# Sums over w_o rows for two tokens: accumulated in PSUM, half of them moved behind a second fetch of the weights

## The chip, the cores and the metric

One core of a Trainium2 chip runs the whole program. The metric is device microseconds of one execution, given as the median of several runs. Beside it stands one execution taken with the hardware profiler; all rows come from that one. Its engines are named PE (TensorE matmuls), PEld (TensorE weight loads), DVE (VectorE), ACT (ScalarE), POOL (GpSimd) and SP (the queue that starts most loads).

## The reference

A block of a streaming encoder works on 16 learned meta tokens followed by 512 tokens of x, with 1024 channels in float32. Two branches (stick-breaking attention and gated linear attention) are projected, gated, added and projected again:

```
mix = (gate_sb * (sb @ w_sb_out) + gate_gla * (o @ w_gla_out)) @ w_o
h = h + rmsnorm(mix)
```

A gated MLP follows, with a causal convolution over three tokens between `hn @ w_ffn_up` and the gelu. The meta tokens are dropped at the end. The convolution looks back two tokens, so of the 16 meta tokens the last two are needed after `mix`: 514 tokens in all.

## The kernel before

**Numbers in parts.** Every matmul operand is split into a high part and a low part (`split`, line 136, and `load_w`, line 80): ACT rounds the operand to the high part, and DVE or POOL subtracts it from the operand for the low part. Three matmuls (high-high, high-low, low-high) stand for one. `load_w` starts the transfer on SP into one of three "raw" buffers, casts on ACT (line 89) and subtracts on POOL (line 90). A raw buffer comes free when its last reader is done.

**Order of the work.** A planner orders the instructions of each engine from a model of their times, with the order of the program text as priority; on the chip each engine then keeps that order, and waits where an operand or buffer is late. An `issue_after` in the text pins an instruction behind another.

**The stretch around the change.** It starts after the attention stages.

1. Lines 783 to 794, for each of 8 slices j of 128 channels: the attention branch is projected (`proj`, 24 matmuls into one of two PSUM buffers of the tag "mm"), the result is multiplied by its gate (line 786), the other branch `tg` is added (line 787), and the mix is split into `mh[j]` and `ml[j]` (line 137 on ACT, 138 on DVE). Its first two columns, the two last meta tokens, are copied to `m2` (line 791). At odd j the rows of w_o for two slices, columns 512 to 1023, are loaded (`raw_o`) and split into `woh` and `wol`, which stay in SBUF.
2. Lines 884 to 892, the first half of the output projection: for the 512 tokens in four blocks and columns 0 to 511 of w_o, loaded two slices at a time (`raw_oa`), 96 matmuls into the same two "mm" buffers.
3. `second` (line 896): the upper half of the columns, 24 matmuls per token block into the tag "z". `gained` squares a result on ACT (line 821) and multiplies it by the norm's gain on DVE (line 822). `normed` (line 831) makes the two norms of a token block and transposes it by 16 matmuls (line 845) into PSUM tiles of the tag "s", of which there are two.
4. The two meta tokens do not go through these matmuls. `accumulate` (line 774) forms their products on DVE: for each of the 8 slices and each token a row of w_o, 128 x 512, is multiplied by the token's column of `m2` and added to `acc` in SBUF (line 779; the first one is line 781). That is 16 operations for columns 512 to 1023, in the loop of item 1, and 16 for columns 0 to 511, in the loop of item 2. `mini` (line 849) adds `acc` over the partitions by 32 matmuls (line 855) and makes the norms of these two tokens; it is pinned behind the matmuls of `second(3)`.
5. The loads of `w_ffn_up` and `w_ffn_gate` (`raw_up`, `raw_ga`) come next in the same three raw buffers; their first matmuls need the normed tokens.

Of the kernel before, what the change touches and what calls it, by code (L numbers as in the profile page):

```python
# [9 lines left out]
F32 = mybir.dt.float32  # L10
# [3 lines left out]
ALU = mybir.AluOpType  # L14
PSUM = bass.MemoryType.PSUM

P = 128
D = 1024
KT = D // P
NM = 16  # L20
# [3 lines left out]
T0 = 14  # L24
# [26 lines left out]
def block_kernel(ctx: ExitStack, tc: tile.TileContext, x, meta_tokens, norm_mix_pre, w_in, w_gk_up, b_gk,  # L51
# [3 lines left out]
    pe, act, dve, pool, sp = nc.tensor, nc.scalar, nc.vector, nc.gpsimd, nc.sync  # L55

    x = x[0]
    out = out[0]
    w_in, w_gk_up, w_sb_out, w_gla_out, w_o = w_in[0], w_gk_up[0], w_sb_out[0], w_gla_out[0], w_o[0]
# [6 lines left out]
    wp = ctx.enter_context(tc.tile_pool(name="wp", bufs=3))  # L66

    def mmt(name):
        return psm.tile([P, 1024], F32, tag="mm", name=name)

    def pst(name, tag="s"):
        return pss.tile([P, 512], F32, tag=tag, name=name)
# [5 lines left out]
    last_raw = [None]  # L78

    def load_w(src, nk, name, hi_out=None, lo_out=None, lo_eng=pool, into=None):  # L80

        ncol = src.shape[-1]
        raw = wp.tile([P, nk, ncol], F32, tag="raw", name=f"raw_{name}")
        sp.dma_start(raw, src)
        last_raw[0] = raw
        if hi_out is None:
            hi_out = (into or wp).tile([P, nk, ncol], F32R, tag="wh", name=f"wh_{name}", bufs=2)
            lo_out = (into or wp).tile([P, nk, ncol], F32R, tag="wl", name=f"wl_{name}", bufs=2)
        act.copy(hi_out, raw)  # L89
        lo_eng.tensor_tensor(out=lo_out, in0=raw, in1=f32(hi_out), op=ALU.subtract)  # L90
        return hi_out, lo_out

    def cols(w, c0, n=P):
        return w[:, c0 : c0 + n].rearrange("(k p) m -> p k m", p=P)

    def wrows(w, k0, nk, c0, c1):
        return w[k0 * P : (k0 + nk) * P, c0:c1].rearrange("(k p) m -> p k m", p=P)

    def proj(w, xh, xl, segs, name, apart=False):

        wh, wl = w
        nk, m = wh.shape[1], wh.shape[2]
        (l0, l1), (_, l2) = segs
        pt = mmt(f"pt_{name}")
        segs = [(pt[:m, 512 - l1 + l0 : 512], l0, l1), (pt[:m, 512 : 512 + l2 - l1], l1, l2)]
        steps = [(k, a, b) for k in range(nk) for a, b in ((wh, xh), (wh, xl), (wl, xh))]
        for grp in ([[s] for s in segs] if apart else [segs]):
            for n, (k, a, b) in enumerate(steps):
                for dst, lo, hi in grp:
                    pe.matmul(dst, a[:, k, :], b[:, k, lo:hi], start=n == 0, stop=n == len(steps) - 1)  # L110
        return pt[:m, 512 - l1 + l0 : 512 + l2 - l1]
# [24 lines left out]
    def split(hi, lo, src):  # L136
        act.copy(hi, src)  # L137
        last_low[0] = dve.tensor_tensor(out=lo, in0=src, in1=f32(hi), op=ALU.subtract)  # L138
# [194 lines left out]
    with ExitStack() as pgs:  # L333
# [4 lines left out]
        for h in LEVELS:  # L338
            with tc.issue_after(low4.ins) if h < EASY else ExitStack():
                m = pgc.tile([P, 264], F32, name=f"mk{h}")  # L340
# [24 lines left out]
        with tc.tile_pool(name="plr", bufs=2) as plr:  # L365
# [30 lines left out]
            for c, (t, n) in enumerate(CHUNKS):  # L396
# [4 lines left out]
                e = plr.tile([P, 512], F32, tag="e", name=f"e{c}", bufs=5)  # L401
# [181 lines left out]
    tg = pm.tile([P, 8, TQ], F32, name="tg")  # L583
    with tc.tile_pool(name="pa", bufs=1) as pa:
# [169 lines left out]
        gates, mh, ml = {}, {}, {}  # L754
# [16 lines left out]
    m2 = pr.tile([P, 8, NM - T0], F32, name="m2")  # L771
    acc = pr.tile([P, NM - T0, D], F32, name="acc")

    def accumulate(k0, c):
        for kk in range(2):
            for t in range(NM - T0):
                w, m = last_raw[0][:, kk, :], m2[:, k0 + kk, t : t + 1]
                if k0 + kk:
                    dve.scalar_tensor_tensor(out=acc[:, t, c], in0=w, scalar=m, in1=acc[:, t, c], op0=ALU.mult, op1=ALU.add)
                else:  # L780
                    dve.tensor_scalar(out=acc[:, t, c], in0=w, scalar1=m, scalar2=None, op0=ALU.mult)

    for j in range(8):
        e = pr.tile([P, TQ], F32, tag="e", name=f"mix{j}", bufs=2)
        pt = proj(load_w(cols(w_sb_out, j * P), 4, f"so{j}"), sbh, sbl, LATE, f"so{j}")
        dve.tensor_tensor(out=e, in0=pt, in1=gates[j], op=ALU.mult)
        dve.tensor_tensor(out=e, in0=e, in1=tg[:, j, :], op=ALU.add)
        mh[j] = pe_.tile([P, TQ], F32R, tag=f"mh{j}", name=f"mh{j}")
        ml[j] = pe_.tile([P, TQ], F32R, tag=f"ml{j}", name=f"ml{j}")
        split(mh[j], ml[j], e)  # L790
        dve.tensor_copy(m2[:, j, :], e[:, : NM - T0])
        if j % 2:
            load_w(wrows(w_o, j - 1, 2, 512, D), 2, f"o{j}", hi_out=woh[:, j - 1 : j + 1, :], lo_out=wol[:, j - 1 : j + 1, :])
            accumulate(j - 1, slice(512, D))
    p1.close()


# [11 lines left out]
    with tc.tile_pool(name="pw", bufs=1) as pw:  # L809
# [39 lines left out]
        def mini():  # L849

            nt = NM - T0
            tp = pst("mini")
            for k in range(KT):
                for t in range(nt):
                    pe.matmul(tp[:, nt * k + t : nt * k + t + 1], acc[:, t, k * P : (k + 1) * P], ones[:, 0:1], start=True, stop=True)
            z = tp[:, : nt * KT].rearrange("p (k t) -> p k t", t=nt)

            def rstd(src, nm):
                s = pw.tile([P, KT, nt], F32, tag="msq", name=f"msq{nm}")
                act.activation(s, src, AF.Square)  # L860
                tp = pst(f"ms{nm}")
                yield
                pe.matmul(tp[:, : nt * KT], ones, s.rearrange("p k t -> p (k t)"), start=True, stop=True)
                ss = pw.tile([P, nt], F32, tag="mss", name=f"mss{nm}")
                dve.tensor_reduce(out=ss, in_=tp[:, : nt * KT].rearrange("p (k t) -> p t k", t=nt), op=ALU.add, axis=mybir.AxisListType.X)
                return rstd_of(pw, ss, D, nm).unsqueeze(1).broadcast_to([P, KT, nt])

            h = pw.tile([P, KT, nt], F32, name="hm")
            dve.tensor_tensor(out=h, in0=z, in1=g1T.unsqueeze(2).broadcast_to([P, KT, nt]), op=ALU.mult)
            dve.tensor_tensor(out=h, in0=h, in1=(yield from rstd(z, "mix0")), op=ALU.mult)  # L870
            dve.tensor_tensor(out=h, in0=h, in1=mT.rearrange("p t k -> p k t"), op=ALU.add)
            g = pw.tile([P, KT, nt], F32, name="hmg")
            dve.tensor_tensor(out=g, in0=h, in1=g2T.unsqueeze(2).broadcast_to([P, KT, nt]), op=ALU.mult)
            dve.tensor_tensor(out=g, in0=g, in1=(yield from rstd(h, "ffn0")), op=ALU.mult)
            split(h2h[:, :, SEQ:], h2l[:, :, SEQ:], g)
            yield
# [4 lines left out]

        pos = [mmt("wo01"), mmt("wo23")]
        d0 = [pos[i // 2][:, (i % 2) * 512 : (i % 2) * 512 + 512] for i in range(4)]
        for k in range(8):
            if k % 2 == 0:
                wh, wl = load_w(wrows(w_o, k, 2, 0, 512), 2, f"oa{k}")
                accumulate(k, slice(0, 512))
            a, b = wh[:, k % 2, :], wl[:, k % 2, :]
            for i in range(4):
                t = slice(i * P + NM - T0, i * P + P + NM - T0)  # L890
                for q, (m, w) in enumerate(((mh, a), (mh, b), (ml, a))):
                    pe.matmul(d0[i], m[k][:, t], w, start=k == 0 and q == 0, stop=k == 7 and q == 2)  # L892

        last_mm = [None]

        def second(i):
            t = (i - 1) * P + NM - T0
            ops = [(m[k][:, t : t + P], w[:, k, :]) for k in range(8) for m, w in ((mh, woh), (mh, wol), (ml, woh))]
            pt = pst(f"wob{i}", "z")
            for q, (a, b) in enumerate(ops):  # L900
                after = sum(q >= c for c in CUT) if i == 4 else 0
                with tc.issue_after(last_ht[after].ins) if after else ExitStack():
                    last_mm[0] = pe.matmul(pt, a, b, start=q == 0, stop=q == len(ops) - 1)
            return pt
# [4 lines left out]
        m = mini()  # L909
        for i in (2, 3, 4):  # L910
            pt = second(i)
# [24 lines left out]
    with tc.tile_pool(name="pu", bufs=2) as pu:  # L936
        for m in range(FT):
            pt = proj(load_w(cols(w_up, m * P), KT, f"up{m}", into=wx if m % 2 else None), h2h, h2l, FFNS, f"up{m}", apart=m < 2)
# [8 lines left out]
            for r, d in ((1, 1), (0, 2)):  # L947
                c = cw[:, r, m : m + 1]
# [223 lines left out]
```

## Time and profile before

| what | us |
|---|---|
| median of 3 runs (968.11 to 970.13) | 969.35 |
| the profiled execution | 969.08 |
| its span, first to last instruction | 967.3 |

| engine | busy us | share of the span |
|---|---|---|
| PE | 938.5 | 97% |
| PEld | 866.3 | 90% |
| DVE | 661.5 | 68% |
| ACT | 488.9 | 51% |
| POOL | 357.6 | 37% |

The mean granted clock of TensorE over the span was 0.992 of full speed. The stretch of items 1 and 2 lies between 508 and 574 us of the span; mini's matmuls start at 586.74 and the first matmul of the MLP at 596.00. A busy share is a mean over all stages, so a stretch is read by its own rows: who is busy there, and what ended the others' idle time.

### The profile page before, as it was taken

What the parts mean: (1) busy time and instruction counts of PE and PEld (TensorE: products, weight loads), DVE (VectorE), ACT (ScalarE), POOL (GpSimd) and SP (SyncE); (2) the same over time, 40 slices, a digit from 0 to 9 for tenths busy, and PEclk for the clock granted to TensorE, in tenths of its full rate; (3) what the DMA queues carried; (4) which work ended last, traced back from release to release, by engine and by line L of the source; (5) the groups of instructions that cost most, each with busy time, mean ns of one, the idle gap of its engine ahead of it and who ended that gap; (6) DMA issues with size and microseconds to landing.
All of it is one profiled execution on the core that took longest, in us unless ns stands there. A gap on an engine that the chain in (4) does not pass through costs nothing.

```text
span 967.3 us, 16621 instructions
## 1 busy us (share of the span) xinstructions
PE 938.5 (97%) x6588; PEld 866.3 (90%) x6588; DVE 661.5 (68%) x1110; ACT 488.9 (51%) x913; POOL 357.6 (37%) x268
## 2 busy tenths in 40 slices
PE   7999999999999998999999899999999999999996
PEld 7999999999999998999998678998999999988775
DVE  6675867767557877777858967554545554478897
ACT  5664554546377565665754235433333333355654
POOL 6523232222244554444545452444444444200200
PEclk9999999999999999999999999999999999999999
DMA  7122212221222321232213364233333233364923
GB/s 216 45 66 66 66 45 66 66 66 44 67 66 67 86 68 45 65 88 58 75 55 90 117 207 140 61 112 93 89 92 104 87 88 94 103 237 167 254 86 127
DMA packets 129727, 92.79 MB, mean 96 GB/s; under 512 B 4064, under 2 KB 114914, under 8 KB 129650
## 3 DMA queue, kind: packets, MB, share of 16 engines
q1 hardware_dynamic: 126178, 82.55, 28.8%
q0 software_dynamic: 1504, 2.88, 1.8%
q10 hardware_dynamic: 1968, 6.29, 1.8%
q8 instruction: 52, 0.85, 0.4%
q14 instruction: 25, 0.20, 0.1%
HBM read 87.52 MB, written 4.19 MB: 95 GB/s over the span
## 4 chain that ended last, share of the span: by engine, by line
PE 83%; DVE 10%; issue 2%; ACT 2%; POOL 2%; DMA 1%; DVEq 0%; ACTq 0%; POOLq 0%
PE pt_up L110 13%; PE ga L958 13%; PE pt_gr L110 5%; PE pt_gv L110 5%; PE pt_go L110 4%; PE pt_mg L110 4%; PE dA L1020 3%; PE pt_ms L110 3%; PE dD L1020 3%; PE pt_gk L110 2%; PE dB L1020 2%; PE wo L892 2%; PE pt_gq L110 2%; PE pt_sv L110 2%; PE pt_sk L110 2%
## 5 line engine op out<-in xcount | busy, mean ns | idle before, releaser
L90 POOL TENSOR_TENSOR wl_up<-raw_up,wh_up 128x1024 fp32r<-128x1024 f32 x22 | 53.0, 2409 | 68.3 <-ACT wh_up L89 68.3
L90 POOL TENSOR_TENSOR wl_ga<-raw_ga,wh_ga 128x1024 fp32r<-128x1024 f32 x22 | 55.2, 2509 | 56.6 <-ACT wh_ga L89 56.6
L110 PE MATMUL pt_up<-h2l,wh_up 128*128 128x256 f32 (+1 forms) x352 | 73.6, 283 | 0.3 <-DVE h2l L207 0.2
L110 PE MATMUL pt_up<-h2h,wh_up 128*128 128x256 f32 (+1 forms) x352 | 73.6, 283 | 0.2
L110 PE MATMUL pt_up<-h2h,wl_up 128*128 128x256 f32 (+1 forms) x352 | 73.3, 282 | 0.0
L958 PE MATMUL ga<-h2h,wl_ga 128*128 128x512 f32 (+1 forms) x192 | 72.2, 376 | 0.0
L958 PE MATMUL ga<-h2l,wh_ga 128*128 128x512 f32 (+1 forms) x192 | 72.2, 376 | 0.0
L958 PE MATMUL ga<-h2h,wh_ga 128*128 128x512 f32 (+1 forms) x192 | 72.0, 375 | 0.0
L89 ACT CAST wh_up<-raw_up 128x1024 fp32r<-128x1024 f32 x22 | 23.0, 1049 | 85.8 <-PE pt_up L110 76.2
L110 PEld LDWEIGHTS pt_up<-h2h,wh_up 128*128 128x128 f32 x352 | 56.9, 189 | 2.2 <-ACT h2h L206 0.5
L110 PEld LDWEIGHTS pt_up<-h2l,wh_up 128*128 128x128 f32 x352 | 55.5, 189 | 0.7 <-DVE h2l L207 0.7
L110 PEld LDWEIGHTS pt_up<-h2h,wl_up 128*128 128x128 f32 x352 | 55.3, 189 | 0.0
L958 PEld LDWEIGHTS ga<-h2h,wl_ga 128*128 128x128 f32 x192 | 36.2, 189 | 7.0
L949 DVE SCALAR_TENSOR_TENSOR cy<-pt_up,cw,cy 128x511 f32<-128x511 f32 (+1 forms) x22 | 16.4, 745 | 37.7 <-ACT cy L946 37.7
L958 PEld LDWEIGHTS ga<-h2l,wh_ga 128*128 128x128 f32 x192 | 36.2, 188 | 6.2
L958 PEld LDWEIGHTS ga<-h2h,wh_ga 128*128 128x128 f32 x192 | 36.2, 189 | 6.1
L949 DVE SCALAR_TENSOR_TENSOR yp<-pt_up,cw,yp 128x511 f32<-128x511 f32 (+1 forms) x22 | 16.4, 745 | 30.9 <-ACT yp L946 30.9
L89 ACT CAST wh_ga<-raw_ga 128x1024 fp32r<-128x1024 f32 x22 | 23.0, 1048 | 25.3 <-PE ga L958 24.8
L1048 POOL DMA_DIRECT2D tv<-in_w_ffn_down_dram x6 | 7.1, 1183 | 68.1 <-DVE wl_p L138 68.1
L90 POOL TENSOR_TENSOR wl_gr<-raw_gr,wh_gr 128x1024 fp32r<-128x1024 f32 x8 | 19.0, 2372 | 35.9 <-ACT wh_gr L89 33.1
L137 ACT CAST sh_p<-As 128x512 fp32r<-128x512 f32 (+1 forms) x30 | 17.4, 583 | 29.3 <-PE dB L1020 12.5
L90 POOL TENSOR_TENSOR wl_gv<-raw_gv,wh_gv 128x1024 fp32r<-128x1024 f32 x7 | 16.9, 2416 | 38.0 <-ACT wh_gv L89 38.0
(558 smaller groups left out, 3261.3 us busy)
## 6 DMA issues: line engine op xcount, KB each, us to landing
raw_up<-in_w_ffn_up_dram SPq DMA_DIRECT2D x22, 512.0 KB, 3.9
raw_ga<-in_w_ffn_gate_dram SPq DMA_DIRECT2D x22, 512.0 KB, 3.8
raw_t<-in_w_ffn_down_dram SPq DMA_DIRECT2D x10, 512.0 KB, 7.3
raw_gv<-in_w_in_dram SPq DMA_DIRECT2D x8, 512.0 KB, 3.9
raw_gr<-in_w_in_dram SPq DMA_DIRECT2D x8, 512.0 KB, 3.9
raw_mg<-in_w_in_dram SPq DMA_DIRECT2D x8, 512.0 KB, 3.9
raw_go<-in_w_gla_out_dram SPq DMA_DIRECT2D x8, 512.0 KB, 4.1
raw_ms<-in_w_in_dram SPq DMA_DIRECT2D x8, 512.0 KB, 4.0
```

The lines of the kernel that those rows point to most:

```text
L89: act.copy(hi_out, raw)
L90: lo_eng.tensor_tensor(out=lo_out, in0=raw, in1=f32(hi_out), op=ALU.subtract)
L110: pe.matmul(dst, a[:, k, :], b[:, k, lo:hi], start=n == 0, stop=n == len(steps) - 1)
L137: act.copy(hi, src)
L892: pe.matmul(d0[i], m[k][:, t], w, start=k == 0 and q == 0, stop=k == 7 and q == 2)
L949: dve.scalar_tensor_tensor(out=y[:, d:], in0=pt[:, : SEQ - d], scalar=c, in1=y[:, d:], op0=ALU.mult, op1=ALU.add)
L958: pe.matmul(pg_[:, lo:hi], a[:, k, :], b[:, k, lo:hi], start=lo == 0 and k == 0 and q == 0, stop=k == KT - 1 and q == 2, skip_group_check= ...
L1020: mm[i] = pe.matmul(dsts[i], a, b, start=first and k == 0 and j == 0, stop=last and k == NP - 1 and j == 2, skip_group_check=True)
L1048: return lambda n, q, nk: pool.dma_start(out=t[:, q : q + nk, :], in_=block(s, c, q, nk), accum_op=ALU.add)
```

## The change

`accumulate` now takes a list of raw tiles with their slice numbers and a range of columns. It adds into two PSUM tiles of the tag "s", one for each token, and copies them to `acc` by ACT at the end. It is called twice, both times after the loop of the first-half projection: once with the four `raw_oa` tiles, and once with four new raw tiles (`raw_ob`), for which the rows of w_o, columns 512 to 1023, are fetched a second time on SP. The call in the first loop is gone. In that loop the gating product is written back to its PSUM tile, and the sum with `tg` reads it there.

```diff
-    def accumulate(k0, c):
-        for kk in range(2):
-            for t in range(NM - T0):
-                w, m = last_raw[0][:, kk, :], m2[:, k0 + kk, t : t + 1]
-                if k0 + kk:
-                    dve.scalar_tensor_tensor(out=acc[:, t, c], in0=w, scalar=m, in1=acc[:, t, c], op0=ALU.mult, op1=ALU.add)
-                else:
-                    dve.tensor_scalar(out=acc[:, t, c], in0=w, scalar1=m, scalar2=None, op0=ALU.mult)
+    def accumulate(raws, c):
+
+        to = [pst(f"ac{c.start}_{t}") for t in range(NM - T0)]
+        for k0, raw in raws:
+            for kk in range(2):
+                for t in range(NM - T0):
+                    w, m = raw[:, kk, :], m2[:, k0 + kk, t : t + 1]
+                    if k0 + kk:
+                        dve.scalar_tensor_tensor(out=to[t], in0=w, scalar=m, in1=to[t], op0=ALU.mult, op1=ALU.add)
+                    else:
+                        dve.tensor_scalar(out=to[t], in0=w, scalar1=m, scalar2=None, op0=ALU.mult)
+        for t in range(NM - T0):
+            act.copy(acc[:, t, c], to[t])

     for j in range(8):
...
-        dve.tensor_tensor(out=e, in0=pt, in1=gates[j], op=ALU.mult)
-        dve.tensor_tensor(out=e, in0=e, in1=tg[:, j, :], op=ALU.add)
+        dve.tensor_tensor(out=pt, in0=pt, in1=gates[j], op=ALU.mult)
+        dve.tensor_tensor(out=e, in0=pt, in1=tg[:, j, :], op=ALU.add)
...
-            accumulate(j - 1, slice(512, D))
...
+        raws = []
         for k in range(8):
             if k % 2 == 0:
                 wh, wl = load_w(wrows(w_o, k, 2, 0, 512), 2, f"oa{k}")
-                accumulate(k, slice(0, 512))
+                raws.append((k, last_raw[0]))
...
+        accumulate(raws, slice(0, 512))
+        again = []
+        for k in range(0, 8, 2):
+            again.append((k, wp.tile([P, 2, 512], F32, tag="raw", name=f"raw_ob{k}")))
+            sp.dma_start(again[-1][1], wrows(w_o, k, 2, 512, D))
+        accumulate(again, slice(512, D))
```

## Rows read from the trace of the kernel before

**Rows 1.** The page, busy time of each engine: us (share of the span), instructions.

```profile
PE 938.5 (97%) x6588; PEld 866.3 (90%) x6588; DVE 661.5 (68%) x1110; ACT 488.9 (51%) x913; POOL 357.6 (37%) x268
```

**Rows 2.** Timeline of PE: start, us, instruction, count, [idle before, releaser].

```profile
544.51 0.74 PE L903 MATMUL wob<-woh,ml 128*128 128x512 f32 x2 [3.05 <-DVE ml L138]
...
546.65 0.77 PE L892 MATMUL wo<-wh_oa,mh 128*128 128x512 f32 x1 [0.72 <-ACT wh_oa L89]
...
573.48 0.39 PE L892 MATMUL wo<-wh_oa,ml 128*128 128x512 f32 x1
...
582.99 2.05 PE L845 MATMUL ht<-drffn,hb 128*128 128x128 f32 x16
...
586.74 3.63 PE L855 MATMUL mini<-ones,acc 128*128 128x1 f32 x32
```

**Rows 3.** Busy us by stretch: length; PE, PEld, DVE, ACT, POOL; granted clock, DMA.

```profile
508.00:572.50 64.50, 58.57 (x333) 49.81 (x333) 55.12 (x67) 19.96 (x30) 31.86 (x15) 0.97 0.46 143
...
511.60:565.20 53.60, 47.67 (x272) 40.30 (x271) 53.15 (x66) 16.36 (x23) 28.19 (x14) 0.97 0.45 144
...
546.60:550.10 3.50, 3.44 (x9) 2.76 (x10) 3.50 (x3) 0.00 (x0) 2.80 (x1) 0.54 0.47 146
550.10:572.50 22.40, 22.40 (x97) 17.91 (x96) 15.76 (x23) 4.25 (x7) 8.65 (x3) 1.00 0.66 212
```

**Rows 4.** Groups on DVE from 508 to 572.5: shapes, count, busy us, mean ns, idle.

```profile
L779 DVE SCALAR_TENSOR_TENSOR acc<-raw_o,m,acc 128x512 f32<-128x512 f32 x14 | 15.2, 1126 | 0.1
L779 DVE SCALAR_TENSOR_TENSOR acc<-raw_oa,m,acc 128x512 f32<-128x512 f32 x14 | 12.0, 890 | 0.0
L138 DVE TENSOR_TENSOR ml<-mix,mh 128x514 fp32r<-128x514 f32 x8 | 9.7, 1213 | 0.0
L787 DVE TENSOR_TENSOR mix<-mix,tg 128x514 f32<-128x514 f32 x8 | 6.2, 779 | 0.1
L791 DVE COPY m<-mix 128x2 f32<-128x2 f32 x8 | 5.6, 701 | 0.2
L786 DVE TENSOR_TENSOR mix<-pt_so,gate 128x514 f32<-128x514 f32 x8 | 5.5, 683 | 0.0
...
L781 DVE TENSOR_SCALAR acc<-raw_oa,m 128x512 f32<-128x512 f32 x2 | 0.9, 474 | 0.0
```

**Rows 5.** Timeline of DVE, columns as in rows 2.

```profile
517.05 3.56 DVE L779 SCALAR_TENSOR_TENSOR acc<-raw_o,m,acc 128x512 f32<-128x512 f32 x2
...
562.53 2.72 DVE L779 SCALAR_TENSOR_TENSOR acc<-raw_oa,m,acc 128x512 f32<-128x512 f32 x4
...
574.91 0.69 DVE L822 TENSOR_TENSOR hb<-wo,g1bc 128x512 f32<-128x512 f32 x1 [9.05 <-ACT wj L821]
```

**Rows 6.** Timeline of POOL.

```profile
517.60 2.46 POOL L90 TENSOR_TENSOR wol<-raw_o,woh 128x1024 fp32r<-128x1024 f32 x1 [1.34 <-ACT woh L89]
```

**Rows 7.** Line 949, the convolution: count, ns min/median/max, first and last start.

```profile
L949 DVE SCALAR_TENSOR_TENSOR yp<-pt_up,cw,yp x22: 739/744/751, 619.7 to 836.6; 128x511 f32<-128x511 f32 x11, 128x510 f32<-128x510 f32 x11
```

**Rows 8.** Waits of the SP queue, 498 to 600: us, times, longest.

```profile
SPq L84 <- DVE acc L779: 34.6, 7, 8.9
```

**Rows 9.** The instructions on mix, columns as in rows 7.

```profile
L787 DVE TENSOR_TENSOR mix<-mix,tg x8: 680/682/1074, 512.3 to 553.7; 128x514 f32<-128x514 f32 x8
```

**Rows 10.** Busy us by stretch of line 110 alone: length, PE, PEld, clock, DMA.

```profile
508.00:572.50 64.50, 23.93 (x193) 23.39 (x192) 0.97 0.46 143
```

**Rows 11.** Transfers, 530 to 600 and 562 to 568: KB, us to landing; one issue.

```profile
raw_oa<-in_w_o_dram SPq DMA_DIRECT2D x4, 512.0 KB, 3.7
...
raw_up<-in_w_ffn_up_dram SPq DMA_DIRECT2D x2, 512.0 KB, 5.5
...
567.54 0.37 SPq L84 DMA_DIRECT2D raw_up<-in_w_ffn_up_dram  x1
```

**Rows 12.** Timeline of ACT, columns as in rows 2.

```profile
572.30 2.00 ACT L89 CAST wh_up<-raw_up 128x1024 fp32r<-128x1024 f32 x2 [9.57 <-DMA raw_up<-in_w_ffn_up_dram]
574.20 0.59 ACT L821 ACTIVATE wj<-wo 128x512 f32<-128x512 f32 x1
```

## The prediction

> **What bounds the kernel now.** I read the page's busy line first, then busy times by stretch, then the waits inside the stretch that the change touches. Over the whole span TensorE is busy 97% [rows 1], so only a stretch where it is not the limit can give anything. The touched stretch runs from the first branch projection (508 us) to the end of the first-half output projection, whose last matmul starts at 573.48 [rows 2]. There VectorE is busy 53.15 of 53.60 us, and TensorE 58.57 of 64.50: 5.9 us idle [rows 3]. The idle time lies in five gaps from 530 to 546.6; the longest, 3.05 us, ends at VectorE's ml, the last, 0.72, at a weight cast [rows 2]. After the gaps the granted clock is 0.54: 9 matmuls take 3.50 us (0.39 each), against 97 in 22.40 (0.231 each) behind them [rows 3]. [...] So VectorE sets this stretch, and TensorE loses 5.9 + 1.4 = **7.3 us** by it.
>
> Why VectorE is so long: the sums over w_o rows are 15.2 + 12.0 + 0.9 + 0.9 = 29.0 us there [rows 4]. One goes at 0.68 us when undisturbed (four in 2.72), but two took 3.56 at 517.05 while POOL's subtraction of 517.60 ran for 2.46 us [rows 5, 6]: 3.56 - 2 x 0.68 = 2.2 us more than their length, and they end half a microsecond behind that subtraction. The same can be read from the means: operations with every operand in SBUF (sums, mix + tg, the 2-column copy, the ml subtraction) are above their short length, while the gating product, which reads PSUM, is flat at 683 ns [rows 4]. A scalar_tensor_tensor of nearly the same shape with one PSUM input and an SBUF pointer scalar, the convolution's, stays within 739 to 751 ns in all 22 cases [rows 7].
>
> **The change, part by part.** (1) *Sums of the upper half leave the first loop.* Sixteen operations go, the raw_o groups: 15.2 + 0.9 = 16.1 us of VectorE [rows 4]. The raw_o buffers come free after the cast and POOL's subtraction alone; the load queue waits 34.6 us in all for these and the other sums today [rows 8].
>
> (2) *Sums of the lower half go to PSUM.* 16 operations, today 12.0 + 0.9 us. No row shows VectorE writing PSUM, so I bound it. Nearest below: no change, 0.68 us each, as reads of PSUM show (683 ns); a gain below that I exclude, as the undisturbed SBUF form takes the same time. The first operation, a tensor_scalar at 474 ns [rows 4], I price at 0.68 as well. Upper end: it waits as now, 3.56 / 2 = 1.8 each. I take 0.68, nearest to the form of rows 7: 16 x 0.68 = 10.9 us. At the upper end the half would be 28.8 us.
>
> Whether PSUM costs more by itself: the product that reads PSUM takes 683 ns [rows 4], the undisturbed SBUF sum of the same size 680 to 682 [rows 9], so I add nothing. [...]
>
> (3) *The gated product stays in PSUM.* The product is unchanged; mix + tg now has a PSUM input and loses its excess, 6.2 - 8 x 0.68 = 0.8 us [rows 4, 9]. In exchange a projection's PSUM buffer is released one operation later (0.68 us). Two buffers alternate and one projection takes 24 matmuls, 24 x 0.124 = 3.0 us (23.93 us for 193 [rows 10]), so 2 x 0.68 hides under the next projection as long as VectorE is at hand. If a stalled ml subtraction stands in front (up to the 2.2 us seen above), it shows for about 1 us.
>
> (4) *What stays.* The ml subtraction (9.7 us) and the 2-column copy (5.6 us) keep all operands in SBUF, so 9.7 - 8 x 0.68 = 4.3 us of the one and up to the whole 5.6 of the other (0.70 apiece for two columns) remain waits [rows 4].
>
> VectorE in the stretch afterwards: product 5.5, sum with tg 5.4, ml 9.7, copy 5.6, lower sums 10.9 = 37.1 us, and 48.0 with the upper sums too. TensorE needs 64.5 - 7.3 = 57.2. So TensorE becomes the limit and the end of the first-half projection moves from 573.9 to about 566.6. Even at the upper end of (2) the lower half fits: 5.5 + 5.4 + 9.7 + 5.6 + 28.8 = 55.0.
>
> (5) *Upper sums again, from weights fetched twice.* Four more transfers of 512 KB on SP, put in front of raw_up and raw_ga: each 3.7 us to landing when alone, 5.5 beside the 2 MB read of x [rows 11]. Each holds one of three raw buffers for landing plus 4 sums, 3.7 + 2.7 = 6.4 us; four turns over three buffers are 8.5 us of queue. Then 16 sums, 10.9 us, on VectorE, and four ACT copies at about 0.6 us (the squares of the same size). They must end before three things: the first norm step on VectorE (574.91 now [rows 5]), the transposing matmuls (582.99), which need the same two PSUM buffers, and mini (586.74), which reads acc [rows 2]. With buffers no longer held by late sums I place the lower sums' end near 550 and the upper ones' near 561, before 566.6, in VectorE's 57.2 - 48.0 = 9 us of slack. Cover: the first-half matmuls. If it is gone, see the slower rival.
>
> (6) *Behind the stretch.* ACT stands 9.57 us for raw_up, casts twice (2.00) and only then takes the first square, at 574.20 [rows 12]. raw_up's second transfer is issued at 567.54 [rows 11]; it now comes behind four more. I take it as keeping its place relative to the end of the projection.
>
> Sum: 7.3 gained, less 1.2 kept for one exposed stall of (3) and (4) (the mean excess per j, at most (4.3 + 5.6) / 8) = 6.1. The profiled execution took 969.08 us: 963.0. The median of the runs, 969.35, lies 0.27 above it, so for the median: **963.3**.
>
> **The rivals.** *VectorE stays the bound (slower).* Place: the upper sums, ahead of the norms. If the lower sums still end at 565.2 as now [rows 5], two ACT copies (1.2) and 16 sums (10.9) run to 577.3; the first norm step waits from 574.91 to there, +2.4: 971.7. Slow transfers (5.5) add up to some 1.8 for the last one: 973.5. It decides once the upper sums end after the projection does. For it: ml and copy keep their waits, VectorE is full today. Against: 16.1 us leave the stretch, and 9.05 us of VectorE idle time lies just ahead of 574.91 [rows 5].
>
> *ACT's queue keeps the time (same).* If raw_up's second load still lands just before the casts of 572.30 [rows 12], casts and the first square stay where they are, and the gain is spent waiting: 969.1, or 967.5 with a landing 1.6 us earlier. For it: ACT already waits there, and 8.5 us of queue come in front. Against: the 34.6 us that SP waits for sums shrink by more.
>
> *More than forecast.* The planner orders ACT by modelled times; with raw_up later it may put the squares ahead of the casts: 2.0 more and no kept stall, 963.3 - 2.0 - 1.2 = 960.1.
>
> *The change doesn't do what it says.* Sums in PSUM wait for POOL all the same. Rows 7 speak against it, and (4) shows that the stretch would still fit at 55.0; it merges into the first rival through (5): 16 x 1.8 = 28.8 us of upper sums would end far behind 566.6.
>
> **How the numbers follow.** Forecast 0.58, more 0.12, same 0.16, slower 0.14 (0.04 of it the last rival). A measurement of this kernel can tell about 0.2%, 1.9 us. Faster: 0.58 + 0.12 = 0.70; within 0.2%: 0.16; slower: 0.14. The range runs from 959.6 (the better case, its 960.1 less half a microsecond for the runs' spread) to 970.0, which takes in no change and leaves out most of the slower rival. The forecast's own range is 960.5 to 967.4: from nothing kept to an added 4 us of exposed waits.
>
> **What would show it.** Right: in the page's groups the sums near 0.7 us with no long ones and mix + tg at 0.68; TensorE's gaps between 530 and 547 gone and no stretch at 0.54 of the clock; first-half projection ending near 567; four raw_ob transfers landing before it; sums of the upper half done before the first square. Wrong: VectorE still full until 565, a long wait of ACT for raw_up, transposing matmuls or mini waiting for VectorE sums or ACT copies, or sums in PSUM above 1 us.

## The result, and the profile after

The changed kernel takes 974.17 us (median of 4 runs, 973.89 to 974.8); the kernel before, run with it, 968.87. The ratio is 1.005 [1.0034, 1.0066]: slower by half a per cent, where 963.3 and a gain were forecast. The profiled execution took 973.89 us with a span of 972.2, against 969.08 and 967.3: 4.9 us of span to explain.

The page's busy line, against [rows 1]:

```profile
PE 941.4 (97%) x6588; PEld 870.5 (90%) x6588; DVE 654.1 (67%) x1110; ACT 490.9 (50%) x917; POOL 352.2 (36%) x268
```

VectorE has 7.4 us less to do, as meant. TensorE is busy 2.9 us longer with the same 6588 matmuls, so some of them ran slowly. Groups on VectorE from 508 to 572.5, columns as in [rows 4]:

```profile
L782 DVE SCALAR_TENSOR_TENSOR ac<-raw_oa,m,ac 128x512 f32<-128x512 f32 x14 | 9.9, 748 | 0.0
L782 DVE SCALAR_TENSOR_TENSOR ac<-raw_ob,m,ac 128x512 f32<-128x512 f32 x14 | 9.4, 754 | 1.5 <-DMA raw_ob<-in_w_o_dram 1.5
...
L791 DVE TENSOR_TENSOR pt_so<-pt_so,gate 128x514 f32<-128x514 f32 x8 | 5.6, 695 | 2.0 <-PE pt_so L110 2.0
L792 DVE TENSOR_TENSOR mix<-pt_so,tg 128x514 f32<-128x514 f32 x8 | 5.5, 688 | 0.1
```

Here the change does what it says. The sums no longer wait for POOL: 9.9 and 9.4 us where [rows 4] had 15.2 and 12.0, and mix + tg is flat. Two sums take 1.41 us at 539.23 although a POOL subtraction runs from 538.85 for 2.36 us; two of them beside such a subtraction took 3.56 before [rows 5, 6]. What went wrong is when the sums run. VectorE's timeline with that POOL row, then TensorE's (columns as in [rows 2]):

```profile
537.31 1.41 DVE L784 TENSOR_SCALAR ac<-raw_oa,m 128x512 f32<-128x512 f32 x2 [5.04 <-DMA raw_oa<-in_w_o_dram]
...
539.23 1.41 DVE L782 SCALAR_TENSOR_TENSOR ac<-raw_oa,m,ac 128x512 f32<-128x512 f32 x2
...
563.85 8.00 DVE L782 SCALAR_TENSOR_TENSOR ac<-raw_ob,m,ac 128x512 f32<-128x512 f32 x12 [1.48 <-DMA raw_ob<-in_w_o_dram]
```

```profile
538.85 2.36 POOL L90 TENSOR_TENSOR wl_oa<-raw_oa,wh_oa 128x1024 fp32r<-128x1024 f32 x1
```

```profile
541.38 0.48 PE L110 MATMUL pt_so<-sbh,wh_so 128*128 128x258 f32 x2 [3.08 <-DVE mix L792]
...
572.81 0.40 PE L897 MATMUL wo<-wh_oa,ml 128*128 128x512 f32 x1
...
582.73 0.51 PE L914 MATMUL wob<-woh,mh 128*128 128x512 f32 x1 [4.63 <-DVE hb L826]
...
586.03 2.17 PE L849 MATMUL ht<-drffn,hb 128*128 128x128 f32 x16
```

The fourth upper block (the upper half of the columns for the fourth 128 tokens) starts at 582.73 after a wait of 4.63 us. In the kernel before, this block waited 1.68 us:

```profile
580.90 0.49 PE L903 MATMUL wob<-woh,mh 128*128 128x512 f32 x1 [1.68 <-DVE hb L822]
```

At 537.31 VectorE has stood 5.04 us at the first lower sum, because raw_oa had not landed; the gating of the next projections waits behind it, and TensorE then stands 3.08 us. The upper sums end at 563.85 + 8.00 = 571.85. What hangs on that end is in SP's issues and in ACT's timeline:

```profile
531.68 9.92 SPq L84 DMA_DIRECT2D raw_oa<-in_w_o_dram  x4
549.38 14.55 SPq L903 DMA_DIRECT2D raw_ob<-in_w_o_dram  x4
566.61 0.37 SPq L84 DMA_DIRECT2D raw_up<-in_w_ffn_up_dram  x1
...
571.88 0.37 SPq L84 DMA_DIRECT2D raw_up<-in_w_ffn_up_dram  x1
```

```profile
571.37 1.05 ACT L89 CAST wh_up<-raw_up 128x1024 fp32r<-128x1024 f32 x1 [9.72 <-DMA raw_up<-in_w_ffn_up_dram]
572.32 1.06 ACT L786 COPY acc<-ac 128x512 f32<-128x512 f32 x2
573.28 0.61 ACT L825 ACTIVATE wj<-wo 128x512 f32<-128x512 f32 x1
...
576.53 1.05 ACT L89 CAST wh_up<-raw_up 128x1024 fp32r<-128x1024 f32 x1 [0.93 <-DMA raw_up<-in_w_ffn_up_dram]
577.49 0.59 ACT L825 ACTIVATE wj<-wo 128x512 f32<-128x512 f32 x1
...
578.92 0.60 ACT L825 ACTIVATE wj<-wo 128x512 f32<-128x512 f32 x1 [0.67 <-DVE hb L826]
```

ACT's fourth square before, with no cast between the four (the first at 574.20 [rows 12]):

```profile
577.84 0.60 ACT L821 ACTIVATE wj<-wo 128x512 f32<-128x512 f32 x1 [0.67 <-DVE hb L822]
```

The raw buffer of the last sum is free at 571.88, and raw_up's second load is issued in that moment, 4.34 us later than before [rows 11]. ACT's order was fixed with this cast ahead of the third square, so the third square waits for a transfer that has nothing to do with it. The chain that ended last says the same (start, us, what):

```profile
568.46 3.40 DVE ac L782 x5
571.88 4.63 DMA raw_up<-in_w_ffn_up_dram
...
579.11 0.93 DVE a_mix L131
```

The last line is a second loss by the same cast: a 128x1 operation of the norm took 0.93 us on VectorE (0.18 in the chain of the kernel before) and ended with the POOL subtraction of the weights just cast (577.66 to 580.01). So the fourth square is 1.08 us late, and the fourth upper block 1.83 (582.73 for 580.90).

Busy us by stretch (columns as in [rows 3]) show the clock, first of the changed kernel, then of the kernel before:

```profile
272.00:275.50 3.50, 3.50 (x22) 3.43 (x21) 0.00 (x0) 1.76 (x6) 2.36 (x1) 0.57 0.02 5
508.00:572.50 64.50, 60.68 (x354) 53.28 (x353) 48.75 (x68) 21.89 (x34) 28.51 (x17) 0.97 0.52 169
...
582.70:586.10 3.40, 3.37 (x9) 2.66 (x10) 2.59 (x11) 1.57 (x6) 0.00 (x0) 0.55 0.55 199
593.00:601.20 8.20, 7.12 (x31) 6.28 (x30) 5.85 (x7) 1.42 (x3) 3.59 (x3) 0.58 0.60 192
```

```profile
272.00:275.50 3.50, 3.50 (x33) 3.48 (x32) 0.42 (x2) 2.45 (x8) 2.65 (x2) 1.00 0.02 5
...
580.90:583.00 2.10, 2.10 (x9) 1.44 (x9) 1.62 (x8) 1.29 (x5) 0.00 (x0) 1.00 0.82 306
588.00:596.00 8.00, 7.87 (x48) 7.30 (x47) 6.35 (x12) 2.91 (x7) 5.31 (x3) 0.79 0.37 108
```

Length times (1 - granted clock), worked out from these rows, is my estimate of what a stretch loses: 1.5 us more at 272, 1.5 more after the wait of 4.63 (nothing before, where the wait was 1.68), and 3.4 against 1.7 ahead of the first up matmuls. The matmuls say much the same after the wait: 9 in 3.40 us, where the kernel before has 9 in 2.10.

Where the 4.9 us went, as the difference between like instructions of the two traces:

| TensorE or ACT at | before | after | difference | added by this part |
|---|---|---|---|---|
| first pt_so matmul | 507.94 | 509.80 | +1.86 | +1.86 |
| last first-half matmul | 573.48 | 572.81 | -0.67 | -2.53 |
| fourth square on ACT | 577.84 | 578.92 | +1.08 | +1.75 |
| first transposing matmul | 582.99 | 586.03 | +3.04 | +1.96 |
| mini | 586.74 | 589.90 | +3.16 | +0.12 |
| span | 967.3 | 972.2 | +4.9 | +1.74 |

So the touched stretch did gain, 2.53 us; 1.86 were lost ahead of every changed line, and 5.6 behind the stretch.

### The profile page after: what moved, and what is told of

Its sections match the earlier page's. It is cut to its first block, busy times and chain, and to the rows that moved or that the text cites. A ratio compares the mean times of both kernels' runs of the same rounds, so it can differ in the third digit from the quotient of the medians.

```text
span 972.2 us, 16635 instructions
## 1 busy us (share of the span) xinstructions
PE 941.4 (97%) x6588; PEld 870.5 (90%) x6588; DVE 654.1 (67%) x1110; ACT 490.9 (50%) x917; POOL 352.2 (36%) x268
## 4 chain that ended last, share of the span: by engine, by line
PE 79%; DVE 10%; DMA 4%; issue 3%; POOL 2%; ACT 1%; DVEq 0%; SPq 0%; POOLq 0%; ACTq 0%
PE pt_up L110 13%; PE ga L969 13%; PE pt_gr L110 5%; PE pt_gv L110 5%; PE pt_mg L110 4%; PE pt_go L110 4%; PE pt_ms L110 3%; PE dA L1031 3%; PE pt_gk L110 2%; PE pt_sv L110 2%; PE pt_gq L110 2%; PE pt_sk L110 2%; PE dB L1031 2%; PE pl L476 2%; PE pt_sq L110 2%
```

## The experiments

Not all of these kernels ran on the same chip, so times are compared by their ratio to the kernel before on the same chip. The changed kernel ran with the first set only; with the others, all but one execution of the kernel before lie between 967.9 and 972.6 us (medians 970.1 to 970.7), so a difference of two ratios is uncertain by about 0.002. Each trace is one execution.

| kernel | median us | ratio to before |
|---|---|---|
| changed kernel | 974.17 | 1.005 [1.0034, 1.0066] |
| gate_only | 970.27 | 1.0002 [0.999, 1.0014] |
| no_upper_sums | 966.7 | 0.9967 [0.995, 0.9984] |
| up_casts_last | 969.62 | 0.9995 [0.9981, 1.0009] |
| low_sums_last | 966.96 | 0.9958 [0.9941, 0.9974] |
| both_last | 970.9 | 1.0002 [0.999, 1.0013] |
| one_fetch | 982.64 | 1.0128 [1.0111, 1.0144] |
| one_fetch_casts_last | 980.05 | 1.0101 [1.0083, 1.0118] |
| old_casts_last | 975.57 | 1.0052 [1.0038, 1.0067] |
| after_filled | 972.49 | 1.0024 [1.0008, 1.0039] |
| low_sums_last_filled | 966.52 | 0.9966 [0.9953, 0.9979] |

### One part alone: the gating (gate_only)

The kernel before with the gated product left in PSUM, nothing else.

```diff
-        dve.tensor_tensor(out=e, in0=pt, in1=gates[j], op=ALU.mult)
-        dve.tensor_tensor(out=e, in0=e, in1=tg[:, j, :], op=ALU.add)
+        dve.tensor_tensor(out=pt, in0=pt, in1=gates[j], op=ALU.mult)
+        dve.tensor_tensor(out=e, in0=pt, in1=tg[:, j, :], op=ALU.add)
```

> The kernel before with the gating product written back to PSUM and mix + tg reading it there, sums as before. By my prediction 0.8 us of VectorE's excess goes and the PSUM buffer is held one operation longer; VectorE stays full, so a change of -1 to +1 us. It also tells whether the 1.9 us that the changed kernel is late before the changed lines (from 271 us on) come back in a kernel whose text there is the same.

No difference from before, as expected. VectorE's time in the stretch fell from 55.12 [rows 3] to 51.70 us, and TensorE did no more in it (58.36 against 58.57). Less work on the bounding engine was not yet a gain: TensorE still stood 2.50 us for a single ml. The late start of the changed kernel shows here in part, with the old text ahead of it: the granted clock is 0.50 from 272 to 274 and 0.90 from 274 to 276, and the first pt_so matmul starts at 508.68, 0.74 later than before.

### One part taken out: the upper sums (no_upper_sums)

```diff
         for t in range(NM - T0):
             act.copy(acc[:, t, c], to[t])
+            act.copy(acc[:, t, 512:], to[t])
...
-        accumulate(again, slice(512, D))
```

The second fetch goes too; the upper half of `acc` for the two tokens is a copy of the lower, so that part of the output is not computed.

> The changed kernel without the second fetch and without the sums of the upper half; the upper half of acc is filled with the lower half's sums by two more ACT copies, so two tokens' upper columns are left out. It bounds what the second fetch and its sums cost. If they are what costs (they occupy the raw buffers and VectorE up to 571.9), raw_up lands some 8 us earlier, the squares start when the projection ends, and the time falls below the kernel before: 963 to 967. If the loss lies elsewhere (the lower queue order, the earlier 1.9 us), it stays above 970.

raw_up was cast twice from 565.65, the first square came at 570.05 and the fourth at 573.70, and the wait of 4.63 us at the fourth upper block shrank to 0.75. The median lies within the 963 to 967 expected. By the ratios the upper sums cost the changed kernel 0.0083, 8 us. The profiled spans differ by 8.9 (963.3 for 972.2), of which 1.67 lie ahead of the stretch (first pt_so at 508.13): this execution met no fall of the clock at 272 (1.00 from 272 to 276). The gain of the stretch is there once nothing ends late.

### ACT's order (up_casts_last)

```diff
+            with tc.issue_after(first_half.ins) if m < 2 else ExitStack():
+                w = load_w(cols(w_up, m * P), KT, f"up{m}", into=wx if m % 2 else None)
```

`first_half` is the last square of the first half; the first two raw_up casts come behind it.

> The changed kernel, with the casts of the first two raw_up tiles pinned on ACT behind the four squares of the first-half projection. Theory Q (ACT's queue): the stretch itself gains some 2.6 us, and it is given away because ACT's squares stand behind casts that wait for raw_up (9.7 us in front of the first square, 0.9 us and a cast of 1.0 in front of the third). Then the first square starts at or before 572.3 - 1.1 and the four come in one row; the two norms start 2 to 3 us earlier and the time is 970.5 to 972.0 against 974.2. Theory S (the sums themselves: VectorE's upper sums end at 571.9 and the norms come after them): the norms' products on VectorE can't start before the sums end, and the time stays within 1 us of 974.2.

5.3 us came back by the ratios, all of the loss against before and more than either theory allowed. In the traces it is 4.0 us of span (968.2 for 972.2), from the same start (first pt_so at 509.81 and 509.80), so all of it lies behind that. ACT's timeline:

```profile
571.65 1.25 ACT L786 COPY acc<-ac 128x512 f32<-128x512 f32 x2 [10.10 <-DVE ac L782]
572.79 0.61 ACT L827 ACTIVATE wj<-wo 128x512 f32<-128x512 f32 x1
...
576.45 0.60 ACT L827 ACTIVATE wj<-wo 128x512 f32<-128x512 f32 x1 [0.67 <-DVE hb L828]
...
577.04 1.98 ACT L89 CAST wh_up<-raw_up 128x1024 fp32r<-128x1024 f32 x2
```

The first square comes only 0.5 us earlier, not the 2 that theory Q had, as the copies of the upper sums now stand ahead of it. But the four squares take 3.66 us instead of 5.64, and TensorE's wait at the fourth upper block falls from 4.63 to 2.38; no fall of the clock follows it (1.00 from 575 to 585). The transposing matmuls then stand 2.00 us for the norm, so that mini starts 1.7 us earlier (588.23). What came on top lies behind mini: the first up matmul starts 4.1 us earlier (597.18 for 601.24), without the changed kernel's wait of 1.08 ahead of its last transposing matmuls, and with 1.7 us lost to the clock by the same estimate (0.90 from 585 to 595, 0.93 from 595 to 605) in place of 3.4.

### VectorE's order (low_sums_last)

```diff
+        last_mix = dve.tensor_tensor(out=e, in0=pt, in1=tg[:, j, :], op=ALU.add)
...
+        with tc.issue_after(last_mix.ins):
+            accumulate(raws, slice(0, 512))
```

> The changed kernel, with the lower sums pinned on VectorE behind the last mix + tg. Theory H (head of the line): the 5.0 us in which VectorE stood at the first lower sum waiting for raw_oa, and the 3.1 us that TensorE then waited for mix + tg, both go, with the half clock behind them; the first-half projection ends 3 to 4 us earlier. By theory Q the total moves by less than 1.5 us all the same, since ACT still waits for raw_up, which waits for the upper sums. A rival: the sums come later, so their buffers do, and raw_up lands later still: 975 to 977.

The lowest ratio (that of no_upper_sums, 0.9967, can't be told from it), and faster than both kernels. The span fell by 6.4 us (the median by 7.2) and not by less than 1.5: theory Q had raw_up as late as ever, but its second load was issued at 570.13, 1.75 us earlier, since the upper sums ended earlier too. TensorE has no wait at all left from 525 to the end of the projection, and the clock is whole:

```profile
508.00:572.50 64.50, 63.82 (x373) 55.46 (x372) 52.76 (x70) 23.54 (x38) 30.72 (x17) 1.00 0.53 173
```

First pt_so to the last first-half matmul takes 568.12 - 509.72 = 58.40 us; before, 65.54. That is 7.1 us, the forecast's 7.3. Behind it the second raw_up cast (574.97) still stands ahead of the fourth square (575.92), and TensorE still stands 4.70 us at the fourth upper block, and the span is 1.5 shorter than before's from a start 1.8 later: of the 7.1 some 3.8 are given back.

### Both orders (both_last)

Both edits together.

> The changed kernel with the lower sums ordered behind the last gating of a mixed token on VectorE, and the first two raw_up casts ordered behind the last square of the first half on ACT. Theory H+Q (two separate losses, VectorE's queue standing at the first lower sum and ACT's queue standing at the second raw_up cast): the gains add where they do not overlap. With the lower sums last alone the fourth square ended its issue at 575.92 with a cast of raw_up ahead of it; four squares take 3.66 from first to fourth once no cast stands between them, so the fourth comes near 574.2, 1.7 earlier, and the end follows: 964.5 to 965.8 us against 966.96. Rival S (after the first loss is gone the weights of the up stage, not the squares, set the start of the up stage): no gain over the lower sums alone, 966.5 to 967.5 us.

The gains did not add; theory H+Q falls, and with 970.9 so does rival S. The first square moved to 564.54 and the fourth to 569.84 (2.1 us of that are an earlier start of the stretch, first pt_so at 507.59), but the casts, now behind them, stand ahead of the squares of the second half, and TensorE waits 2.16 at the fourth upper block and 1.77 more ahead of the transposing matmuls. The clock of those stretches:

```profile
573.00:584.00 11.00, 9.23 (x31) 7.55 (x32) 8.17 (x20) 7.59 (x21) 4.16 (x3) 0.53 0.57 193
587.00:594.00 7.00, 6.53 (x28) 6.04 (x29) 4.84 (x9) 0.96 (x3) 1.90 (x2) 0.51 0.69 221
```

By the same estimate, which counts TensorE's idle time in them (1.77 and 0.47 us) too, that loses 11 x 0.47 + 7 x 0.49 = 8.6 us. The profiled execution (967.96) was the quickest of twelve; why the median lies 3 above it is open.

### Is the second fetch needed? (one_fetch, one_fetch_casts_last)

All sums in PSUM, the upper ones in the first loop from raw_o as the kernel before makes them, no second fetch; then the same with ACT's order as above.

```diff
+            accumulate([(j - 1, last_raw[0])], slice(512, D), upper, j == 7)
...
-        accumulate(again, slice(512, D))
```

> All sums kept in PSUM but no second fetch: the upper sums are made in the first loop from raw_o, as the kernel before makes them in SBUF, the lower ones behind them from raw_oa. VectorE has the same 32 sums at 0.68 us as the changed kernel, in another place; the transfer of raw_up no longer waits for sums that end behind the projection. Theory T (what the change gained is the sums' speed in PSUM, what it lost is the second fetch's late end): squares start as in the kernel without upper sums, 966 to 968 us. Rival B (VectorE bounds the stretch 508 to 574, so that putting 16 sums, 11 us, back beside the projection's own work gives the idle TensorE time back): 969 to 972 us.

> The kernel with one fetch and all sums in PSUM, and the first two raw_up casts ordered behind the last square of the first half. Theory T: raw_up lands ahead of the squares there, so that ACT's order no longer matters: within 1 us of the same kernel without this order. Rival Q (the casts in front of the squares still cost what they last, 2 casts of about 1 us, whatever lands when): 1.5 to 2.5 us less than without this order.

Both theories of the first missed by 10 us and more. VectorE's timeline, SP's, ACT's and TensorE's:

```profile
551.64 1.40 DVE L786 TENSOR_SCALAR ac<-raw_oa,m 128x512 f32<-128x512 f32 x2
...
561.49 2.73 DVE L784 SCALAR_TENSOR_TENSOR ac<-raw_oa,m,ac 128x512 f32<-128x512 f32 x4 [4.50 <-DMA raw_oa<-in_w_o_dram]
```

```profile
551.19 3.59 SPq L84 DMA_DIRECT2D raw_oa<-in_w_o_dram  x2
```

```profile
549.86 0.45 ACTq L821 DMA_DIRECT2D xr<-in_x_dram  x1
...
561.49 1.05 ACT L89 CAST wh_oa<-raw_oa 128x1024 fp32r<-128x1024 f32 x1 [9.74 <-DMA raw_oa<-in_w_o_dram]
```

```profile
562.59 0.73 PE L901 MATMUL wo<-wh_oa,mh 128*128 128x512 f32 x2 [3.27 <-ACT wh_oa L89]
...
603.99 2.08 PE L853 MATMUL ht<-drffn,hb 128*128 128x128 f32 x8 [3.12 <-DVE ygh L205]
```

The tag "s" has two PSUM buffers, so the lower pair of sums starts only when the upper pair is done and copied, at 551.64; in the kernel before the two lie in SBUF and overlap. Until then sums hold all three raw buffers, two with raw_oa and one with the last raw_o, whose last upper sum ends at 551.13. SP issues raw_oa's third load at 551.19, behind the 2 MB of x (549.86) in place of ahead of it. It lands 10 us later, the projection itself starves, and the first square comes at 581.06. So by these rows the second fetch is what makes two PSUM buffers enough: the projection no longer waits for sums of the other half. More PSUM buffers with one fetch were not tried.

With the casts behind the squares 2.6 us came back, near rival Q's 1.5 to 2.5, but not by its mechanism. Without that order ACT has done both casts by 577.92 and then stands 3.14 us for TensorE ahead of the first square; with it the four squares come only 0.35 us earlier (the fourth at 584.36 for 584.71), and the fourth upper block even 0.5 later (588.29 for 587.75). The gain lies behind mini: the wait of 3.12 us at 603.99 is gone, and the first up matmul starts at 605.81 instead of 608.67. Neither theory had that.

### The old kernel with ACT's order (old_casts_last)

> The kernel before, unchanged but for the first two raw_up casts ordered behind the last square of the first half. Before, the casts at 572.30 waited 9.57 us for raw_up and the first square issued at 574.20, 0.7 us behind the last matmul of the projection at 573.48. Theory: the order on ACT costs the old kernel at most the 1 to 1.9 us between 572.30 and 574.20, so 967.5 to 969.5 us against 969 to 970.7. Rival (the old kernel had the same loss in full): 964 to 966 us.

Slower by 5 us, which neither theory had; the profiled span is 6.6 longer. The work ahead of the stretch is 1.6 late (first pt_so at 509.52), as much as the clock accounts for by the same estimate: 0.57 from 8 to 12 us, 4 x 0.43 = 1.7, far ahead of the edit, where before it was 1.00. The clock was also 0.57 from 547 to 555 and 0.52 from 595 to 602. The edit itself brought little: the fourth square comes at 578.92 for 577.84, so 0.5 earlier by its own start, and the two casts from 579.51 then stand ahead of the second half's squares (581.39, before 578.56); TensorE waits 1.91 us ahead of the transposing matmuls. In the changed kernel, where a square waits for a late transfer, the same order paid. How much of the 5 us is the clock's own course isn't settled.

### What the wait costs beyond itself (after_filled, low_sums_last_filled)

Sixteen matmuls whose result nobody reads, between the third and the fourth upper block, in the wait. To place them the third block moves ahead of the first norm in the program text.

```diff
+            if i == 2:
+                third = second(3)
+                tp = pst("keep")
+                for _ in range(16):
+                    with tc.issue_after(last_mm[0].ins):
+                        last_mm[0] = pe.matmul(tp, mh[0][:, NM - T0 : NM - T0 + P], woh[:, 0, :], start=True, stop=True)
```

> The changed kernel with 16 matmuls whose result nobody reads, put on TensorE between the last matmul of the third upper block (577.70) and the fourth block's first (582.73), where TensorE waits 4.63 us for VectorE. At 0.233 us each they take 3.7 us, less than the wait, and nothing waits for them. Theory C (the wait is paid twice, the second time as the half clock that follows it: eight matmuls from 582.73 at 0.43 us apart in place of 0.23, and a longer half-clock stretch from 593): the clock stays whole behind 582.7, 1.7 us come back there and up to 1.7 at 593 to 600: 970.8 to 972.6 us. Rival W (the wait alone is the loss and the clock falls for another reason): 974 to 975.5 us, the clock behind 582.7 as before.

> The kernel with the lower sums last, and the same 16 unread matmuls in its own wait of 4.70 us (573.4 to 578.10). Theory C: the half clock of 575.98 to 582.8 goes or shrinks, 1.7 to 3.4 us come back against 966.96: 963.5 to 965.3 us, faster than either kernel. Rival W: 966.5 to 968 us.

TensorE's timeline and one stretch of the filled changed kernel:

```profile
577.59 3.90 PE L932 MATMUL keep<-woh,mh 128*128 128x512 f32 x16
582.41 0.50 PE L914 MATMUL wob<-woh,mh 128*128 128x512 f32 x1 [0.93 <-DVE hb L826]
...
595.93 2.07 PE L849 MATMUL ht<-drffn,hb 128*128 128x128 f32 x8 [2.61 <-ACT msqmix L864]
```

```profile
582.70:586.10 3.40, 3.28 (x21) 2.62 (x21) 2.59 (x10) 1.26 (x6) 0.00 (x0) 1.00 0.43 164
```

With the wait filled the clock behind it is whole, 1.00 for 0.55, in the one profiled execution of each; that speaks for the idle time as what made it fall here. The median, 972.49, lies inside theory C's range, 1.7 us below the changed kernel's; but the nine runs go from 970.8 to 974.7 and the two ratios' intervals overlap, so the gain in time is not clear of noise. In the two profiled executions the span falls by 0.8 only, 0.47 of it ahead of the stretch (first pt_so at 509.33), as a part is lost to a longer wait for msqmix (2.61 for 1.08). In the kernel with the lower sums last the fill brought nothing that can be told (966.52 against 966.96; ratios 0.9966 and 0.9958), although its clock is whole as well (1.00 from 573.8 to 585, for 0.51 from 575.9 to 582.8): there the transposing matmuls then wait for the norm,

```profile
581.92 2.02 PE L849 MATMUL ht<-drffn,hb 128*128 128x128 f32 x16 [0.90 <-ACT r_mix L119]
```

and start no earlier than without the fill (581.68), in an execution whose projection also ended 0.6 us later. Rival W had the time of that one right, though the clock did recover: there the norm, and not the clock, ended last.

## Why the prediction was wrong

The sum had 6.1 us of gain; the profiled execution, forecast at 963.0, took 973.89. Of these 10.9 us, 3.6 are the stretch (2.53 us gained in place of 6.1), 1.9 lie ahead of it and 5.6 behind it, where the sum allowed nothing.

**The bound and the 7.3 us: right.** Without the wait at 537.31 the stretch gave 7.1. The 1.4 us in it for the clock are the difference of two lengths in [rows 3]: 3.50 us for 9 matmuls at a granted 0.54, and 9 x 0.231 = 2.1 us at 1.00.

**(1) and (2), the sums: right.** Twelve in a row take 8.00 us, 0.67 apiece, for the 0.68 that I took. What PSUM added in the traces: the product kept there has 695 ns against 683 with SBUF as its target, mix + tg 688 against an undisturbed 680 to 682, and the first operation of each half, the tensor_scalar, 750 against 474 [rows 4]; I had priced that one at 0.68 us as well.

**(3), the PSUM buffer held longer: right.** VectorE waits for TensorE's pt_so now, 2.0 us. But the 1.2 us that I kept for one exposed stall was the wrong term. The stall was **not a slow operation but VectorE's queue standing**: 5.04 us at a sum whose load takes 5.6 us to land (issued at 531.68), planned ahead of the next gating. I listed what each operation costs and not what stands behind each new wait for a transfer. It cost 3.08 us of TensorE and a lower clock behind it (0.62 from 541 to 545.5), and it is most of the difference between 2.53 and 7.1. Taking it away (low_sums_last) gave that back.

**(4), what stays: right.** ml is 9.2 us, the copy 4.9 for two columns each.

**(5), the upper sums' place: wrong.** I put the lower sums' end near 550 and the upper ones' near 561; they were 556.46 and 571.85. The lower ones began late, as told. The second fetch then waited 11.8 us for sums and 5.4 for POOL to free raw buffers, since a raw_oa buffer is read by POOL as well as by the sums. Its four issues spread over 14.55 us, where I had put four turns at 8.5; each load landed in 4.7.

**(6), raw_up: the step that failed.** "I take it as keeping its place relative to the end of the projection." It did not: its second load hangs on the last upper sum through the raw ring, so it was issued 4.34 us later while the projection ended 0.67 earlier. ACT's fixed order passed that on to the squares, the squares to TensorE's wait of 4.63, and the clock behind that wait was 0.55 (1.00 with the wait filled). With ACT's order changed (up_casts_last) the ratio is 0.9995, and without the stall of (3) it is 0.9958, so either of the two orders alone takes the loss away.

**The rivals.** *ACT's queue keeps the time* had the place right and the size wrong: I let the load land as now at the latest, which ends at no change. *VectorE stays the bound* had the sign but not the point: the upper sums ended 1.3 us ahead of the projection's end, and yet it was slower, since the raw buffer and not the norm step is what waits for them. No rival priced the clock behind a longer wait.

**A slip in the range.** The lower end of the forecast's own range, 960.5 "from nothing kept", doesn't follow from the sum: with all of the 7.3 us gained it is 969.35 - 7.3 = 962.1. The measured 974.17 lies above the range either way.

**What no step could hold:** 1.86 us at 272, before any changed instruction. The matmuls there come in the same order and at the same spacing in both traces until 272.2; then one granted clock falls and the other does not (0.57 and 1.00 from 272 to 275.5). Two kernels that differ only in ACT's order behind 570 differ there as well, low_sums_last and then both_last (on different chips):

```profile
272.00:275.50 3.50, 3.50 (x21) 3.43 (x20) 0.00 (x0) 1.55 (x5) 2.38 (x1) 0.53 0.00 0
```

```profile
272.00:275.50 3.50, 3.50 (x32) 3.48 (x31) 1.09 (x4) 1.75 (x7) 2.85 (x3) 1.00 0.05 14
```

On one chip no_upper_sums (1.00 from 272 to 274) and up_casts_last (0.54) differ too, with the same text up to line 785. So nothing ties it to what the change does, though it is a part of the measured time. One execution of each kernel was profiled, and the ten runs of up_casts_last alone go from 968.1 to 971.8 us, so whether the kernel, the chip or the execution decides isn't shown. What tips it wasn't tried and stays open.

## What to carry to other kernels

When sums move, follow each buffer that they hold to the next transfer that wants it and to the engine whose fixed order stands behind that transfer: the sums were cheap, the load issued after their last read was not. An operation that waits for a transfer belongs behind the work that is ready: in VectorE's fixed order one sum that waited 5.04 us for raw_oa cost TensorE 3.08, and with the lower sums behind the last gating TensorE had no wait left from 525 to the end of the projection. With the sums in PSUM, and the lower ones ordered behind the last gating, the change is worth 0.9958 [0.9941, 0.9974].

## What was not expected of the hardware

A wait of TensorE was paid twice where the clock fell behind it: 4.63 us of wait were followed by eight matmuls at 0.43 us apart instead of 0.23, and with 16 matmuls that nobody reads, 3.9 us in that wait, the clock behind it was 1.00 in place of 0.55. The wait's length alone doesn't tell: one of 2.16 us in both_last was followed by a granted clock of 0.53, one of 2.38 in up_casts_last by 1.00. And the same instructions at the same spacing met a fall in one profiled execution (0.57 from 272 to 275.5) and not in another (1.00), 1.5 us by the estimate above, so that a difference of 2 us between two kernels is not yet explained by the edit where the clock ahead of it differs.
